# Queries and two gate blocks of a decoder layer's mixer as seven-product pairs, after keys and values

## The chip, the cores and the metric

One core of one Trainium2 chip runs a whole decoder layer as one program. The metric is the device time in microseconds, the median of several runs; a lower time is better. Inputs and output are float32, and the products keep nearly float32 accuracy by splitting each operand in two parts.

## The reference, cut to what matters

The layer is a feed-forward block, a token mixer, a cross-attention and a second feed-forward block on 256 tokens of width 2048. The change lies in the mixer:

```python
h = rms_norm(x, norm_g)                      # 256 x 2048
p = h @ w_in                                 # 2048 x (1024 + 512 + 3360 + 4096)
q, k, v, p_rwkv, gates = jnp.split(p, c, axis=-1)
y_attn = sliding_window_attention(q, k, v, sinks)
y_rwkv = rwkv7_time_mix(p_rwkv, ...)         # a recurrence over the tokens, 16 heads of 64
gate_attn, gate_rwkv = jnp.split(jax.nn.sigmoid(gates), 2, axis=-1)
merged = gate_attn * (y_attn @ w_proj_attn) + gate_rwkv * (y_rwkv @ w_proj_rwkv)
return x + merged @ w_out
```

## The kernel before, in words

**Products.** A product of the 256 tokens with a block of 512 columns goes over the inner dimension in chunks of 128 rows. Every weight chunk is split into `hi` (rounded by ScalarE to the matmul's format, line 365) and `lo` (the rest, VectorE, line 366), and the activations likewise (`xhi`, `xlo`). One elementary product is three matmuls, `hi`x`xhi`, `lo`x`xhi` and `hi`x`xlo` (`times`, lines 442 to 444), each 128 x 512. An *item* is two chunks (`KU`). A block of 2048 rows of weights (`product`) is 8 items, two token halves, 96 matmuls; a block of 1024 rows (`w_proj_attn`, `w_proj_rwkv`) is 4 items and 48 matmuls. Weights arrive by SyncE's DMA queue in `raw` tiles (four buffers) and are split two items ahead (`AHEAD`); a finished product is taken out of its `acc` banks (three) by ScalarE or VectorE.

**Seven products for eight.** In the feed-forward parts two column blocks are formed together (`product_pair`). A chunk pair of two blocks and two token halves is a 2 x 2 by 2 x 2 block product: eight elementary products, or seven by Winograd's scheme, of sums of weights (lines 394 to 397, split in lines 373 and 374) and of sums of activations (`combinations`). Three of eight chunk pairs of a feed-forward block use the seven. The partial results collect in the banks p1, p3, p5 (`mm`), p2, p4, q (`acc`) and p6, p7 (`tr`), which `first`, `middle` and `out` add up.

**The mixer.** Its products follow in a fixed order: two query blocks, keys and values, a small block of 288 columns ("small": decay, rate and gate inputs), two key blocks of the time-mixing branch (k0, k1), then four times an attention gate block and the `w_proj_attn` block it multiplies, then receptances and values (r0, v0, r1, v1), four gate blocks of the other branch (`gr`), four `w_proj_rwkv` blocks that read `yr`, and `w_out`.

**Background work.** Everything that isn't a product is a generator in one of eight groups (`Interleave`): `feat` turns results to features, `attn` holds eight `attend` jobs (two at a time), `ew` runs one job at a time and in order: `decay_and_rate`, `removal_keys` twice, `substitute` (inverts small triangular blocks, 31 steps on VectorE, lines 1187 and 1192), and then for each half `receptances` and `values`. `chain` holds four `pairs` jobs, two at a time: each waits for "inverse" (the end of `substitute`) and for "ready0" or "ready1" (the end of `values`), forms masked products (line 1290), goes through short dependent steps (lines 1327 to 1398) and hands its result to a `finish` job in `norm`: mean sums (line 875), square root, reciprocal (1445), gate matmuls (1457), four elementwise operations (1458 to 1465) and the split into `yrhi`, `yrlo` (635, 636). A product calls `bg.tick()` twice per item (`product_pair` about four times per item of two blocks), and a tick moves the running jobs by one step. A scheduler then places each engine's instructions, by their order of creation and what they depend on.

**Buffers.** Most tiles of the mixer share 23 buffers of 8 KB a partition (`t4`).

Of the kernel before, what the change touches and what calls it, by code (L numbers as in the profile page):

```python
# [7 lines left out]
F32 = mybir.dt.float32  # L8
# [7 lines left out]
P = 128  # L16
# [21 lines left out]

SEVEN, SEVEN_DOWN = (0, 2, 4), ((2, 4, 6), (2, 4))
SEVEN_2, STAGED = (0, 2, 3, 4), (3,)  # L40

STAGE_AT = [266 + 2 * n for n in range(10)]


class Act:
# [55 lines left out]
def weight_plan(a):  # L101

    w = {n: v[0] for n, v in a.items() if n in _INS}
    yield from feed_forward_plan(w["ffn1_w_gate"], w["ffn1_w_up"], w["ffn1_w_down"], False)
    yield None
    w_in = w["w_in"]
    cols = [0, 512, ATTN_W]
    for c in cols:  # L110
        yield w_in, 0, KD, c, 512
    yield w_in, 0, KD, C_RW + 3 * RW, 288
    for h in range(2):
        yield w_in, 0, KD, C_RW + RW + h * 512, 512
    for n in range(4):
        yield w_in, 0, KD, C_GATE + n * 512, 512
        yield w["w_proj_attn"], 0, 8, n * 512, 512
    for h in range(2):
        yield w_in, 0, KD, C_RW + h * 512, 512
        yield w_in, 0, KD, C_RW + 2 * RW + h * 512, 512  # L120
    for n in range(4):
        yield w_in, 0, KD, C_GATE + D + n * 512, 512
    for n in range(4):
        yield w["w_proj_rwkv"], 0, 8, n * 512, 512
    for n in range(4):
        yield w["w_out"], 0, KD, n * 512, 512
# [10 lines left out]
def decoder_layer(ctx: ExitStack, tc: tile.TileContext, a: dict, out: bass.AP):  # L137
# [19 lines left out]
    def f32(x):  # L157
        return x.bitcast(F32)
# [108 lines left out]

    plan, units, items, ends, staged = [], [], [], [], {}  # L270
    for entry in weight_plan(a):
        if entry is None:
            ends.append(len(units))
            continue
        plan.append(entry)
        w, k0, nk, c0, n = entry
        if not isinstance(w, tuple):
            for k in range(k0, k0 + nk, KU):
                items.append(((len(units),), False))
                units.append((w, k, c0, n))  # L280
            continue
        for k in range(k0, k0 + nk, 2 * KU):
            u = len(units)
            units += [(v, k + i, c, 512) for v, c in zip(w, c0) for i in (0, KU)]
            for i in range(2):
                q = (k - k0) // KU + i
                if n == SEVEN_2 and q in STAGED:
                    staged[len(items)] = len(staged)
                items.append(((u + i, u + 2 + i), q in n))
    raws, parts, summed = {}, {}, {}  # L290
    first_unused = {items[i][0][1] for i in staged}
    sums_d = dram.tile([len(staged), P, 4, 512], F32, name="sums")
    at = {"item": 0, "product": 0, "pool": None}

    def load(u, pieces=None):

        if u >= len(units) or u in raws:
            return
        w, k, c0, n = units[u]
        wide = at["pool"] is not None and (u < ends[0] or u >= ends[1] + LOADED)  # L300
        m = 2 if wide else 1
        if wide:
            raw = at["pool"].tile([P, m * KU, n], F32, tag="raw2", name="raw2", bufs=4)
        else:
            raw = wp.tile([P, KU, n], F32, tag="raw", name="raw", bufs=4)
# [62 lines left out]

    def two_parts(v, e):
        sp = at["pool"]  # L370
        hi = sp.tile([P, KU, 512], F32R, tag="thi" + e, name="thi")
        lo = sp.tile([P, KU, 512], F32R, tag="tlo" + e, name="tlo")
        act.copy(hi[:], v[:])  # L373
        dve.tensor_tensor(lo[:], v[:], f32(hi[:]), ALU.subtract)  # L374
        return hi, lo

    def divide(i):


        if i >= len(items) or i in parts:  # L380
            return
        which, seven = items[i]
        if len(which) == 1:
            parts[i] = split_unit(*which)
            return
        g, u = which
        if not seven:
            parts[i] = split_unit(g), split_unit(u)
            return
        t = summed.get(i)  # L390
        if t is None:
            rg, ru = raws[g], raws[u]
            t = [wp.tile([P, KU, 512], F32, tag="raw", name="raw", bufs=4) for _ in range(2)]
            dve.tensor_tensor(t[1][:, 0], ru[:, 0], rg[:, 0], ALU.subtract)
            dve.tensor_tensor(t[0][:, 0], ru[:, 1], ru[:, 0], ALU.subtract)
            dve.tensor_tensor(t[0][:, 1], ru[:, 1], t[1][:, 0], ALU.subtract)  # L396
            dve.tensor_tensor(t[1][:, 1], rg[:, 1], t[0][:, 1], ALU.subtract)
        a_ = two_parts(t[0], "a")
        parts[i] = split_unit(g), split_unit(u, slice(1, 2)), (a_, two_parts(t[1], "b"))

    def next_item():
        i = at["item"]
        at["item"] += 1
        u = items[i][0][0]
        for v in range(u, u + (2 * LOADED if at["pool"] is not None else LOADED)):
            load(v)
        divide(i)
        room = AHEAD
# [42 lines left out]
                k + i == 0, k + i == nk - 1,  # L451
            )

    def combinations(sp, x: Act, seven, name, ready=lambda: True, early=True, n=0):
# [5 lines left out]
        parts = [sp.tile([P, n, P], F32R, tag=name + e, name=name + e) for e in ("hi", "lo")]  # L460
        c = {"parts": parts, "at": {}, "done": False, "seven": seven, "early": early}

        def work():
# [3 lines left out]
            for q in pairs:  # L467
                while not {2 * q, 2 * q + 1} <= x.done:
                    yield
                t = wp.tile([P, KU, 512], F32, tag="raw", name="raw", bufs=4)  # L470
# [17 lines left out]
                s = slice(o, o + n)  # L488
                with tc.issue_after(at["hi"].ins):
                    act.copy(parts[0][:, s], f[:, :n])  # L490
                yield
                with tc.issue_after(at["lo"].ins):
                    dve.tensor_tensor(parts[1][:, s], f[:, :n], f32(parts[0][:, s]), ALU.subtract)
                c["at"][q] = o
                o += n
                yield
# [5 lines left out]
    def product_pair(x: Act, c, w, first, middle, out):  # L502
# [20 lines left out]
            return [x.at(p, k)[:, t * P : (t + 1) * P] for p in range(2)]  # L523

        def of_c(q, i):
            return [p[:, c["at"][q] + i, :] for p in c["parts"]]

        def of_w(parts_, i):
            return [p[:, i, :] for p in parts_]
# [246 lines left out]
    x3d = dram.tile([T, D], F32, name="x3d")  # L776
    md = dram.tile([T, D], F32, name="md")
    grd = dram.tile([T, D], F32, name="grd")
    ld = dram.tile([P, 32, P], F32, name="ld")
    xd = dram.tile([4, 32, 32, 32], F32, name="xd")  # L780

# [60 lines left out]
    with tc.tile_pool(name="mx", bufs=1, reuse_waits="tile") as sp:  # L842
# [39 lines left out]
                yield  # L882
            bg.seen.add(name)

        qt = []
        for h in range(2):
            tok = scaled(product(n2.x, W["w_in"]), n2.r)
            qt.append(t4("qt"))
            bg.spawn("feat", to_features(tok, qt[h], "q"))

        kd = t4("kd")
        vt = t4("vt", (P, 2, KV_W))
# [2 lines left out]
        for t in range(2):  # L895
# [6 lines left out]
            )  # L902
            act.activation(vt[:, t, :], pb[t][:, KV_W : 2 * KV_W], AF.Copy, scale=n2.r[t])
        bg.spawn("feat", to_features(tok, kd, "kv"))
        ya = act_tiles("ya", 2)
        sink4 = sinks[:].rearrange("p (k c e) -> p k e c", k=4, c=2)

        def attend(kv, qb):
            yield from wait_for("kv")
            w = P * (qb + 1)  # L910
            tq = slice(qb * P, qb * P + P)
            s = t4("s", (P, 2, 2, T))
# [289 lines left out]
        bg.spawn("ew", substitute())  # L1202


        for n in range(4):
            pg = product(n2.x, W["w_in"])
            g = t4("ga", (P, 2, 512))
            for t in range(2):
                act.activation(g[:, t, :], pg[t][:], AF.Sigmoid, scale=n2.r[t])
            pa = product(ya, W["w_proj_attn"])  # L1210
            for t in range(2):
                dve.tensor_tensor(g[:, t, :], pa[t][:], g[:, t, :], ALU.mult)
            pool.dma_start(blk(md, n), g[:])
# [503 lines left out]
```

## Time and profile before

| | |
|---|---|
| median of 3 runs | 2236.56 us (2236.5 to 2237.6) |
| the profiled execution, its own time | 2237.5 us |
| its span, first to last instruction | 2235.6 us |
| mean granted TensorE clock | 0.999 |
| matmuls (TensorE), longest group | 1134 x 3 `acc<-hi,xhi` and its two companions |

How to read the profile: PE is TensorE's matmuls, PEld its weight loads, DVE VectorE, ACT ScalarE, POOL GpSimd, SP SyncE, which issues the weight loads. `out<-in` names what an instruction writes and reads; `x1102` is a count, the next numbers are busy microseconds in all and mean nanoseconds of one. A matmul's row shows it from start to end, and successive matmuls overlap. Lines of `...` leave lines out. A line such as L443 is a line of the kernel before; in the kernel after, the same statements stand 2 to about 70 lines further down (443 is 456, 1290 is 1359, 1445 is 1514).

### The profile page before, as it was taken

How to read it: one execution, taken by the hardware profiler on the slowest of the kernel's cores; microseconds unless marked ns; L12 is line 12 of the kernel's file. 1: busy time of each engine (PE TensorE's matmuls, PEld its weight loads, DVE VectorE, ACT ScalarE, POOL GpSimd, SP SyncE). 2: the span in 40 equal slices, each digit the busy share in tenths (PEclk: the TensorE clock that was granted, in tenths of full speed). 3: DMA queues.
4: the chain of work that ended last, by engine and by line, in shares of the span. 5: the costliest groups of instructions: out<-in, count | busy, mean ns of one | idle time of the engine just before them, and what ended most of it. 6: DMA issues, size and time to landing. Idle time of an engine off the chain costs nothing.

```text
span 2235.6 us, 28143 instructions
## 1 busy us (share of the span) xinstructions
PE 2220.6 (99%) x10520; PEld 1823.4 (82%) x10520; DVE 1823.0 (82%) x2367; ACT 1247.3 (56%) x1625; POOL 121.3 (5%) x181
## 2 busy tenths in 40 slices
PE   9999999999999999999999999999999999999998
PEld 7888888888888877788888888888888888888886
DVE  7999989998989476977657666547999999999997
ACT  7555555555556467544434546556665565655654
POOL 0000000000001001200321030001000000000000
PEclk9999999999999999999999999999999999999999
DMA  8565565556556545687768688658565576556564
GB/s 303 194 210 197 188 209 201 193 190 214 199 189 199 172 134 152 196 232 212 206 215 279 196 260 283 187 160 275 200 243 201 193 242 210 203 206 222 198 227 150
DMA packets 231256, 466.02 MB, mean 208 GB/s; under 512 B 15472, under 2 KB 17616, under 8 KB 231120
## 3 DMA queue, kind: packets, MB, share of 16 engines
q1 hardware_dynamic: 221808, 437.56, 59.0%
q0 software_dynamic: 7648, 23.52, 3.5%
q10 hardware_dynamic: 1664, 3.15, 0.4%
q8 instruction: 82, 1.34, 0.3%
q14 instruction: 54, 0.44, 0.1%
HBM read 440.49 MB, written 23.59 MB: 208 GB/s over the span
## 4 chain that ended last, share of the span: by engine, by line
PE 93%; DVE 3%; DMA 2%; issue 1%; ACT 1%; POOL 0%; SPq 0%; POOLq 0%; ACTq 0%; DVEq 0%
PE acc L442 19%; PE acc L443 18%; PE acc L444 18%; PE mm L444 8%; PE mm L443 8%; PE mm L442 8%; PE tr L443 2%; PE tr L630 2%; PE tr L442 2%; PE tr L444 2%; DVE lo L366 1%; PE mm L1354 1%; PE tr L1290 1%; DMA raw<-in_ffn_w_up_dram 0%; PE mm L917 0%
## 5 line engine op out<-in xcount | busy, mean ns | idle before, releaser
L365 ACT CAST hi<-raw 128x1024 fp32r<-128x1024 f32 (+1 forms) x770 | 755.9, 992 | 701.8 <-PE acc L444 508.7
L366 DVE TENSOR_TENSOR lo<-raw,hi 128x1024 fp32r<-128x1024 f32 (+1 forms) x770 | 881.0, 1147 | 295.2 <-ACT hi L365 293.5
L442 PE MATMUL acc<-hi,xhi 128*128 128x512 f32 (+1 forms) x1134 | 448.3, 396 | 1.4 <-DVE xhi L661 0.6
L443 PE MATMUL acc<-lo,xhi 128*128 128x512 f32 (+1 forms) x1134 | 440.5, 388 | 1.1 <-DVE lo L366 1.1
L444 PE MATMUL acc<-hi,xlo 128*128 128x512 f32 (+1 forms) x1134 | 440.0, 388 | 0.0
L442 PEld LDWEIGHTS acc<-hi,xhi 128*128 128x128 f32 x1134 | 213.2, 188 | 48.5 <-issue 4.9
L443 PEld LDWEIGHTS acc<-lo,xhi 128*128 128x128 f32 x1134 | 213.1, 188 | 44.6 <-DVE lo L366 2.5
L444 PEld LDWEIGHTS acc<-hi,xlo 128*128 128x128 f32 x1134 | 212.9, 188 | 44.1 <-DVE xlo L664 0.5
L373 ACT CAST thi<-raw 128x1024 fp32r<-128x1024 f32 x192 | 199.7, 1052 | 65.3 <-DVE raw L396 44.8
L374 DVE TENSOR_TENSOR tlo<-raw,thi 128x1024 fp32r<-128x1024 f32 x192 | 232.0, 1217 | 1.3 <-ACT thi L373 0.6
L442 PE MATMUL mm<-hi,xhi 128*128 128x512 f32 x402 | 157.9, 393 | 0.1
L444 PE MATMUL mm<-hi,xlo 128*128 128x512 f32 x402 | 156.7, 390 | 0.0
L443 PE MATMUL mm<-lo,xhi 128*128 128x512 f32 x402 | 156.7, 390 | 0.0
L444 PE MATMUL acc<-hi,hlo 128*128 128x512 f32 x372 | 145.5, 391 | 0.0
L443 PE MATMUL acc<-lo,hhi 128*128 128x512 f32 x372 | 145.4, 391 | 0.0
L442 PE MATMUL acc<-hi,hhi 128*128 128x512 f32 x372 | 144.9, 390 | 0.0
L442 PEld LDWEIGHTS mm<-hi,xhi 128*128 128x128 f32 x402 | 75.5, 188 | 15.8 <-ACT hi L365 0.5
L444 PEld LDWEIGHTS mm<-hi,xlo 128*128 128x128 f32 x402 | 75.4, 188 | 15.8
L443 PEld LDWEIGHTS mm<-lo,xhi 128*128 128x128 f32 x402 | 75.5, 188 | 15.4
L443 PEld LDWEIGHTS acc<-lo,hhi 128*128 128x128 f32 x372 | 69.8, 188 | 14.3
L442 PEld LDWEIGHTS acc<-hi,hhi 128*128 128x128 f32 x372 | 69.9, 188 | 14.3
L444 PEld LDWEIGHTS acc<-hi,hlo 128*128 128x128 f32 x372 | 69.9, 188 | 14.0
(394 smaller groups left out, 3567.9 us busy)
## 6 DMA issues: line engine op xcount, KB each, us to landing
raw<-in_ffn_w_down_dram SPq DMA_DIRECT2D x88, 1024.0 KB, 5.2
raw<-in_ffn_w_gate_dram SPq DMA_DIRECT2D x84, 1024.0 KB, 5.2
raw<-in_ffn_w_up_dram SPq DMA_DIRECT2D x78, 1024.0 KB, 6.2
raw<-in_w_in_dram SPq DMA_DIRECT2D x136, 512.0 KB, 3.8
raw<-in_w_out_dram SPq DMA_DIRECT2D x32, 512.0 KB, 4.9
raw<-sums SPq DMA_DIRECT2D x20, 512.0 KB, 6.4
raw<-in_w_proj_attn_dram SPq DMA_DIRECT2D x16, 512.0 KB, 3.8
raw<-in_w_proj_rwkv_dram SPq DMA_DIRECT2D x16, 512.0 KB, 5.9
```

What stands on the lines that cost most here:

```text
L365: at["hi"] = act.copy(hi[:, s], raw[:, s])
L366: at["lo"] = dve.tensor_tensor(lo[:, s], raw[:, s], f32(hi[:, s]), ALU.subtract)
L373: act.copy(hi[:], v[:])
L374: dve.tensor_tensor(lo[:], v[:], f32(hi[:]), ALU.subtract)
L442: pe.matmul(o, xh, hi, start=first, stop=False, **how)
L443: pe.matmul(o, xh, lo, start=False, stop=False, **how)
L444: pe.matmul(o, xl, hi, start=False, stop=last, **how)
L630: pe.transpose(b[:, o : o + P], tok[:, t, col : col + P], ident[:])
L1290: pe.matmul(b[e][:, o : o + P], x1[r, j, cs_], x2[r, j, cs_], start=True, stop=True)
L1354: pe.matmul(vb[:, (o + k) * P : (o + k + 1) * P][:, r], lhs(k, e), rhs[:, k, r], start=first and k + e == 0, stop=True, **ek,)
```

## The change

The mixer's plan and program begin with the keys and values. Then the two query blocks, and after them the first two attention gate blocks, are formed as pairs with seven products for eight in chunk pairs 2, 4 and 6 of eight. The finished gate blocks are stored to memory (`gad`), and each is loaded again where its `w_proj_attn` block is due. The two other gate blocks stay products of one block, each ahead of one of the first two `w_proj_attn` blocks; the last two of these follow at once. Both pairs use combinations of the normalised activations (`cm`), weight sums (`tsum`), their splits and a second set of four load buffers (`raw3`), all kept in the 23 shared buffers for that time. Attention jobs wait for both query blocks. The points at which the second feed-forward block's staged sums are begun move by 16 items, the number of items that the two pairs save.

```diff
+SEVEN_MIX = (2, 4, 6)
-STAGE_AT = [266 + 2 * n for n in range(10)]
+STAGE_AT = [250 + 2 * n for n in range(10)]
...
-    cols = [0, 512, ATTN_W]
-    for c in cols:
-        yield w_in, 0, KD, c, 512
+    yield w_in, 0, KD, ATTN_W, 512
+    for c in (0, C_GATE):
+        yield (w_in, w_in), 0, KD, (c, c + 512), SEVEN_MIX
...
     for n in range(4):
-        yield w_in, 0, KD, C_GATE + n * 512, 512
+        if n < 2:
+            yield w_in, 0, KD, C_GATE + (2 + n) * 512, 512
         yield w["w_proj_attn"], 0, 8, n * 512, 512
...
+        elif u in mix_second:
+            raw = at["mix"]["raw"][sorted(mix_second).index(u) % 4]
...
-        qt = []
-        for h in range(2):
-            tok = scaled(product(n2.x, W["w_in"]), n2.r)
-            qt.append(t4("qt"))
-            bg.spawn("feat", to_features(tok, qt[h], "q"))
+        cm = combinations(sp, n2.x, SEVEN_MIX, "cm", early=False, n=12, room=room)
+
+        def pair_of(w, o, func, done):
+            def first(b):
+                act.copy(o[0][:, 0], b["p1"][:])
+            def middle(b):
+                dve.tensor_tensor(u2, b["p6"][:], o[0][:, 0], ALU.add)
+                dve.tensor_tensor(u3, b["p7"][:], u2, ALU.add)
+                dve.tensor_tensor(u2, b["p5"][:], u2, ALU.add)
+                dve.tensor_tensor(o[1][:, 1], b["q"][:], u3, ALU.add)
+            def out(b, to):
+                t, i = int(to in ("p4", "p5")), int(to in ("p3", "p5"))
+                v = o[i][:, t]
+                e = {"p2": v, "p4": u3, "p3": u2, "p5": v}[to]
+                dve.tensor_tensor(v, b[to][:], e, ALU.add)
+                act.activation(v, v, func, scale=n2.r[t])
+                if t:
+                    done(i)
+            product_pair(n2.x, cm, w, first, middle, out)
...
+        qt = [t4("qt") for _ in range(2)]
+        tok = [t4("tok", (P, 2, 512)) for _ in range(2)]
+        pair_of(W["w_in"], tok, AF.Copy,
+            lambda i: bg.spawn("feat", to_features(tok[i], qt[i], f"q{i}")))
+        ga = [t4("ga", (P, 2, 512)) for _ in range(2)]
+        pair_of(W["w_in"], ga, AF.Sigmoid,
+            lambda i: pool.dma_start(blk(gad, i), ga[i][:]))
...
             yield from wait_for("kv")
+            yield from wait_for("q1")
...
+        gates = []
         for n in range(4):
-            pg = product(n2.x, W["w_in"])
-            g = t4("ga", (P, 2, 512))
-            for t in range(2):
-                act.activation(g[:, t, :], pg[t][:], AF.Sigmoid, scale=n2.r[t])
+            if n < 2:
+                g = t4("ga", (P, 2, 512))
+                gates.append(g)
+                pool.dma_start(g[:], blk(gad, n))
+                pg = product(n2.x, W["w_in"])
+                g = t4("ga", (P, 2, 512))
+                gates.append(g)
+                for t in range(2):
+                    act.activation(g[:, t, :], pg[t][:], AF.Sigmoid, scale=n2.r[t])
             pa = product(ya, W["w_proj_attn"])
+            g = gates[(0, 2, 1, 3)[n]]
             for t in range(2):
                 dve.tensor_tensor(g[:, t, :], pa[t][:], g[:, t, :], ALU.mult)
             pool.dma_start(blk(md, n), g[:])
```

More of the change, by code (lines that the diff above doesn't have):

```diff
@@ L265, in decoder_layer @@
     junk_t = cpool.tile([P, 512], mybir.dt.bfloat16, name="junk")
-    plan, units, items, ends, staged = [], [], [], [], {}
+    plan, units, items, ends, staged, mix_second = [], [], [], [], {}, set()
     for entry in weight_plan(a):
@@ L289, in decoder_layer @@
                 items.append(((u + i, u + 2 + i), q in n))
+            if len(ends) == 1:
+                mix_second.update((u + 2, u + 3))
     raws, parts, summed = {}, {}, {}
@@ L292, in decoder_layer @@
     sums_d = dram.tile([len(staged), P, 4, 512], F32, name="sums")
-    at = {"item": 0, "product": 0, "pool": None}
+    at = {"item": 0, "product": 0, "pool": None, "mix": None}
     def load(u, pieces=None):
@@ L370, in two_parts @@
         sp = at["pool"]
-        hi = sp.tile([P, KU, 512], F32R, tag="thi" + e, name="thi")
-        lo = sp.tile([P, KU, 512], F32R, tag="tlo" + e, name="tlo")
+        if sp is None:
+            hi, lo = at["mix"][e]
+        else:
+            hi = sp.tile([P, KU, 512], F32R, tag="thi" + e, name="thi")
+            lo = sp.tile([P, KU, 512], F32R, tag="tlo" + e, name="tlo")
         act.copy(hi[:], v[:])
@@ L392, in divide @@
             rg, ru = raws[g], raws[u]
-            t = [wp.tile([P, KU, 512], F32, tag="raw", name="raw", bufs=4) for _ in range(2)]
+            if at["pool"] is None:
+                t = at["mix"]["t"]
+            else:
+                t = [wp.tile([P, KU, 512], F32, tag="raw", name="raw", bufs=4) for _ in range(2)]
             dve.tensor_tensor(t[1][:, 0], ru[:, 0], rg[:, 0], ALU.subtract)
@@ L404, in next_item @@
         u = items[i][0][0]
-        for v in range(u, u + (2 * LOADED if at["pool"] is not None else LOADED)):
+        deep = at["pool"] is not None or len(items[i][0]) == 2
+        for v in range(u, u + (2 * LOADED if deep else LOADED)):
             load(v)
@@ L452, in multiply, with combinations @@
             )
-    def combinations(sp, x: Act, seven, name, ready=lambda: True, early=True, n=0):
+    def combinations(sp, x: Act, seven, name, ready=lambda: True, early=True, n=0, room=None):
         pairs = [q for q in range(max(seven) + 1) if early or q in seven]
         n = n or sum(4 if q in seven else 2 for q in pairs)
-        parts = [sp.tile([P, n, P], F32R, tag=name + e, name=name + e) for e in ("hi", "lo")]
+        if room is None:
+            whole = [sp.tile([P, n, P], F32R, tag=name + e, name=name + e) for e in ("hi", "lo")]
+            parts = [lambda o, n, t=t: t[:, o : o + n] for t in whole]
+        else:
+            parts = [
+                lambda o, n, t=t: t[o // 8][:, o % 8 : o % 8 + n] for t in (room[:2], room[2:])
+            ]
         c = {"parts": parts, "at": {}, "done": False, "seven": seven, "early": early}
@@ L469, in work @@
                     yield
-                t = wp.tile([P, KU, 512], F32, tag="raw", name="raw", bufs=4)
+                if room is None:
+                    t = wp.tile([P, KU, 512], F32, tag="raw", name="raw", bufs=4)
+                else:
+                    t = at["mix"]["t4"]("ct", (P, KU, 512))
                 v = t[:, 0].rearrange("p (k t n) -> p k t n", k=2, t=2)
@@ L487, in work @@
                 yield
-                s = slice(o, o + n)
+                hi, lo = (v(o, n) for v in parts)
                 with tc.issue_after(at["hi"].ins):
-                    act.copy(parts[0][:, s], f[:, :n])
+                    act.copy(hi, f[:, :n])
                 yield
                 with tc.issue_after(at["lo"].ins):
-                    dve.tensor_tensor(parts[1][:, s], f[:, :n], f32(parts[0][:, s]), ALU.subtract)
+                    dve.tensor_tensor(lo, f[:, :n], f32(hi), ALU.subtract)
                 c["at"][q] = o
@@ L525, in of_c @@
         def of_c(q, i):
-            return [p[:, c["at"][q] + i, :] for p in c["parts"]]
+            return [p(c["at"][q] + i, 1)[:, 0] for p in c["parts"]]
         def of_w(parts_, i):
@@ L778, in decoder_layer @@
     grd = dram.tile([T, D], F32, name="grd")
+    gad = dram.tile([T, 2 * 512], F32, name="gad")
     ld = dram.tile([P, 32, P], F32, name="ld")
@@ L883, in to_features @@
             bg.seen.add(name)
-        qt = []
-        for h in range(2):
-            tok = scaled(product(n2.x, W["w_in"]), n2.r)
-            qt.append(t4("qt"))
-            bg.spawn("feat", to_features(tok, qt[h], "q"))
+        at["mix"] = {
+            "a": [t4("thi", (P, KU, 512), F32R), t4("tlo", (P, KU, 512), F32R)],
+            "b": [t4("thi", (P, KU, 512), F32R), t4("tlo", (P, KU, 512), F32R)],
+            "t": [t4("tsum", (P, KU, 512)) for _ in range(2)],
+            "raw": [t4("raw3", (P, KU, 512)) for _ in range(4)],
+            "t4": t4,
+        }
+        room = [t4("cm", (P, 8, P), F32R) for _ in range(4)]
+        u2, u3 = (t4("um", (P, 2, 512))[:, i] for i in range(2))
+        cm = combinations(sp, n2.x, SEVEN_MIX, "cm", early=False, n=12, room=room)
[16 more added lines that the diff above has]
+            product_pair(n2.x, cm, w, first, middle, out)
         kd = t4("kd")
@@ L904, in decoder_layer @@
         bg.spawn("feat", to_features(tok, kd, "kv"))
+        qt = [t4("qt") for _ in range(2)]
+        tok = [t4("tok", (P, 2, 512)) for _ in range(2)]
+        pair_of(
+            W["w_in"], tok, AF.Copy,
+            lambda i: bg.spawn("feat", to_features(tok[i], qt[i], f"q{i}")),
+        )
+        ga = [t4("ga", (P, 2, 512)) for _ in range(2)]
+        pair_of(
+            W["w_in"], ga, AF.Sigmoid,
+            lambda i: pool.dma_start(blk(gad, i), ga[i][:]),
+        )
         ya = act_tiles("ya", 2)
```

## The prediction

> **What bounds the kernel now.** I read the page first (busy time, slices, chain), then windows of 20 us, then the instructions of the stretch in which the time-mixing branch meets the merged projection.
>
> ```profile
> span 2235.6 us, 28143 instructions
> PE 2220.6 (99%) x10520; PEld 1823.4 (82%) x10520; DVE 1823.0 (82%) x2367; ACT 1247.3 (56%) x1625; POOL 121.3 (5%) x181
> DVE  7999989998989476977657666547999999999997
> DMA packets 231256, 466.02 MB, mean 208 GB/s; under 512 B 15472, under 2 KB 17616, under 8 KB 231120
> PE 93%; DVE 3%; DMA 2%; issue 1%; ACT 1%; POOL 0%; SPq 0%; POOLq 0%; ACTq 0%; DVEq 0%
> ```
>
> TensorE is busy 99% of the span and is 93% of the chain that ended last. So a matmul taken away shortens the kernel by its spacing, and a microsecond in which TensorE waits lengthens it by one. VectorE is full in the feed-forward parts and half empty in the mixer (slices 13 to 24, about 700 to 1340 us), where the change puts its work. The spacing is read where nothing but products run, at the seam from the last gate product to the first product on `yr`:
>
> ```profile
> 1288.41 0.39 PE L443 MATMUL acc<-lo,xhi 128*128 128x512 f32 x1
> 1288.64 0.39 PE L444 MATMUL acc<-hi,xlo 128*128 128x512 f32 x1
> 1288.87 0.39 PE L442 MATMUL acc<-hi,yrhi 128*128 128x512 f32 x1
> 1289.09 0.39 PE L443 MATMUL acc<-lo,yrhi 128*128 128x512 f32 x1
> ```
>
> Starts lie 0.2267 us apart (0.68 us for three), though each row is 0.39 us long: they overlap. The gate product runs straight into `yr`: nothing waits there now.
>
> ```profile
> core 0: us, PE busy (x) PEld busy (x) DVE busy (x) ACT busy (x) POOL busy (x), PEclk, DMA share, GB/s
> 220.00:240.00 20.00, 20.00 (x90) 16.57 (x89) 19.29 (x25) 10.22 (x11) 0.00 (x0) 1.00 0.56 189
> 740.00:760.00 20.00, 20.00 (x92) 16.54 (x91) 8.57 (x7) 9.03 (x11) 0.00 (x0) 1.00 0.66 186
> 800.00:820.00 20.00, 19.25 (x108) 13.86 (x107) 15.75 (x40) 13.87 (x41) 1.75 (x3) 1.00 0.39 120
> 1100.00:1120.00 20.00, 18.71 (x126) 15.38 (x126) 11.05 (x14) 9.34 (x14) 4.18 (x7) 1.00 0.88 279
> ```
>
> The first row is feed-forward with seven-for-eight pairs: VectorE 19.29 of 20 and TensorE still full. The second is a query product as it is now. The last two hold the idle time of attention (0.75 us) and of the start of the time-mixing chain (1.29 us).
>
> **Part 1, the matmuls removed: -4.1 us.** A chunk pair of two column blocks takes 8 x 3 matmuls, with seven products 7 x 3. Three chunk pairs in each of two pairs of blocks (queries, first gates): 2 x 3 x 3 = 18 matmuls, 18 x 0.2267 = 4.08 us. All are on TensorE's path; nothing else covers them.
>
> **Part 2, VectorE's work in the two pairs: no cost inside, 2.0 us at the seams.**
>
> ```profile
> L366 DVE TENSOR_TENSOR lo<-raw,hi 128x1024 fp32r<-128x1024 f32 x662 | 808.1, 1222 | 288.0 <-ACT hi L365 286.3
> L374 DVE TENSOR_TENSOR tlo<-raw,thi 128x1024 fp32r<-128x1024 f32 x192 | 232.0, 1217 | 1.3 <-ACT thi L373 0.6
> L366 DVE TENSOR_TENSOR lo<-raw,hi 128x512 fp32r<-128x512 f32 x100 | 68.1, 682 | 0.8 <-ACT hi L365 0.8
> L394 DVE TENSOR_TENSOR raw<-raw,raw 128x512 f32<-128x512 f32 x86 | 58.9, 685 | 13.3 <-DMA raw<-in_ffn_w_up_dram 12.7 <-DMA raw<-in_ffn_w_down_dram 0.3
> L581 DVE TENSOR_TENSOR u<-mm,u 128x512 f32<-128x512 f32 x20 | 13.6, 682 | 0.0
> ```
>
> A seven item is 4 x 0.685 + 2 x 1.217 + 1.222 + 0.682 = 7.1 us of VectorE, an eight item 2 x 1.222 = 2.4; three and five of them, with about ten additions from the banks at 0.682, are 40.3 us beside (5 x 24 + 3 x 21) x 0.2267 = 41.5 us of TensorE, 97%. Window 220 to 240 holds the same density, 96%, with TensorE full: inside a pair I charge nothing. If that cover went, 2 to 5 us a pair. The combinations of `n2.x` (nine long and twelve short operations, some 7 us) fall in the keys-and-values product, where VectorE is half idle. At the seams it is tighter: both pairs hold all three `acc` banks (p2, p4 and q), and the bank that the next product needs is freed in `middle`, three additions (2.05 us) after p5, with splits of 1.2 us between. Feed-forward pairs before have no q and start at once. Two seams, from nothing to 2 us each; I take 1 each.
>
> ACT (56% busy) and SP (the same number of 512 KB loads, 16 of them into `raw3`) have room. POOL gets four DMA issues, and 2 MB of store and reload is 0.4% of the 466 MB moved; all this is charged nothing, hidden by products of 21.8 us (96 x 0.2267). The new wait for "q1" costs nothing, since attention is queued behind the gate pair.
>
> **Part 3, what is moved: the time-mixing chain comes later, about 6.7 us.** This sets the sign. Background work advances by one step at each tick, and a product ticks twice an item: 16 times for 2048 rows of weights, 8 times for 1024. Group "ew" runs one job at a time: removal keys, then `substitute`, then `receptances` and `values`, and only behind those can `pairs` begin. From the second key product to the first receptance product there are 4 x 16 + 4 x 8 = 96 ticks now, and 2 x 16 + 4 x 8 = 64 after, because two gate products went ahead of the keys. So the chain comes 32 ticks nearer to its consumer.
>
> ```profile
> L1290 PE MATMUL tr<-at,aa x64: 272/272/373, 1104.7 to 1233.3; 64*128 64x128 f32 x64
> L442 PE MATMUL acc<-hi,yrhi x64: 387/389/482, 1288.9 to 1334.6; 128*128 128x512 f32 x64
> ```
>
> In the built order of instructions, 396 product matmuls stand between the first L1290 and the first `yrhi` product before, 228 after: 168 x 0.2267 = 38 us of cover gone. The end of the chain is what had slack:
>
> ```profile
> 1254.36 0.39 PE L1398 MATMUL tr<-mk,sa 128*64 128x128 f32 x4
> ...
> 1258.89 0.62 PE L875 MATMUL tr<-sp,ones_r 128*128 128x512 f32 x2
> 1259.54 0.69 ACT L1441 ACTIVATE sq<-tr,gneps 128x512 f32<-128x512 f32 x1 [0.76 <-PE tr L875]
> 1260.26 3.35 DVE L1445 RECIPROCAL sq<-sq 128x512 f32<-128x512 f32 x1 [0.23 <-ACT sq L1441]
> 1263.42 0.40 PE L1457 MATMUL tr<-xr,gh 128*128 128x256 f32 x2
> 1263.53 1.16 DVE L366 TENSOR_TENSOR lo<-raw,hi 128x1024 fp32r<-128x1024 f32 x1
> 1264.36 0.39 PE L442 MATMUL acc<-hi,xhi 128*128 128x512 f32 x1
> 1264.61 0.68 DVE L1458 TENSOR_TENSOR yq<-yq,sq 128x512 f32<-128x512 f32 x1
> 1264.69 1.28 ACT L1487 ACT_TABLE_LOAD   x1
> 1265.21 1.22 DVE L366 TENSOR_TENSOR lo<-raw,hi 128x1024 fp32r<-128x1024 f32 x1
> 1266.34 0.87 DVE L1462 SCALAR_TENSOR_TENSOR yq<-yq,cols,bv 128x256 f32<-128x256 f32 x2
> 1267.13 0.86 DVE L1465 SCALAR_TENSOR_TENSOR yq<-yq,cols,tr 128x256 f32<-128x256 f32 x2
> 1268.03 0.62 ACT L635 CAST yrhi<-yq 128x512 fp32r<-128x512 f32 x1
> 1268.68 0.69 DVE L636 TENSOR_TENSOR yrlo<-yq,yrhi 128x512 fp32r<-128x512 f32 x1 [0.69 <-ACT yrhi L635]
> ```
>
> From the last mean sums (L875) to the last `yrlo` is 1269.37 - 1258.89 = 10.5 us, two splits of 1.16 and 1.22 us among them. Bare it is 0.62 + 0.69 + 3.35 + 0.68 + 0.87 + 0.86 + 0.62 + 0.69 = 8.4 us. Before, 162 product matmuls (36.7 us) stand between these sums and the product that reads this block of `yr`. After, the built order has only the sums (0.45 us), the eight gate matmuls of L1457 (0.94 us, 1263.42 to 1264.36) and six product matmuls (1.36 us): 2.75 us. TensorE then waits for `yrhi`, 8.4 - 0.7 - 2.75 = 4.95 us, and after two matmuls some 0.25 for `yrlo`: 5.2 us, or 7.3 if two splits get in again. The built order shows none between the reciprocal and `yrlo`, so I take 5.2. The block before it has about 11 us of cover for a path of the same length plus a table load (1.28) and two splits (2.4), which makes a wait near 0.75; the chain's last copies and the first merged transposes behind it add as much. I take 1.5 for these (0 to 3).
>
> At the start of the chain, the 1.29 us idle at 1100 to 1120 may go or come back (-1.2 to +1.2): nothing charged.
>
> Sum: -4.1 + 2.0 + 5.2 + 1.5 = +4.6 us, so 2242.1 against the profiled execution's 2237.5; the median of the runs is 0.94 lower, so **2241.2 us**.
>
> TensorE's clock column reads 1.00 in every window above, and the worst of them loses 1.3 us in all. The Trainium skill, "TensorE: Matmul & The Clock Gate", section "What's actually happening", says that the array falls to half clock after an idle window of about 3.4 us and needs a busy one as long to come back. By that rule the new 5 us wait would cost an estimated further 1.7 us; no run here shows a pause that long.
>
> **Rivals.** (a) The other side: the tail is covered. If `ready0` came early enough that the last sums stood 40 product matmuls before their consumer (9 us, more than 8.4), no wait arises and the 18 matmuls are all: 2236.6 - 4.1 + (0 to 2) = 2233.5, below 2232.1 only if attention's 0.75 or the chain start's 1.29 us go too. For it: TensorE is full at 1280 to 1300 now. Against: six matmuls in the built order. 15%. (b) VectorE becomes the bound in the two pairs: at 97% any handover between ACT and VectorE (286 us of waits on L365 in all) pushes it over; the first pair also carries the 7 us of combinations. 5 us more: 2246. Against: window 220 to 240. 13%. (c) After the wait the matmuls run slower: twelve of them at double spacing are 2.7 us, half of that 1.4; 2 us more: 2243.2. For it only the length of the pause. 7%. The clock page's rule is this case. (d) The waits just eat the gain, with seams at nothing and the start of the chain smoother: 2237, 5%.
>
> **How the numbers follow.** Forecast 60%, its own range 2238.5 to 2244, a little more than half above +0.2% (2241.0); 0.2% either way is about what a measurement of this kernel tells from no change. Slower: 0.33 + 0.13 + 0.07 = 0.53. Within: 0.27 + 0.07 of (a) + 0.05 = 0.39. Faster: 0.08, the rest of (a). Range: low, tail at 5.2, everything else at its lower end with some of (a), 2235; high, tail 7.3, seams 4, others 3, 2247 with (b).
>
> **What would show it.** Right: eighteen fewer 128x512 matmuls; a TensorE pause of 4 to 8 us before the third and fourth chunk pairs of the first product on `yr`, ended by ACT's `yrhi`; L1290's first start some 35 us later; TensorE full in both pairs. Wrong: no such pause (a); pauses on `lo` or `tlo` inside the pairs (b); PEclk under 1.00 behind the pause (c). A time under 2235 would say that the tail was covered.

## The result, and the profile after

The kernel after takes 2265.45 us (median of 4 runs, 2264.92 to 2268.81) against 2236.61 us before in the same runs: a ratio of 1.0131, 95% interval 1.0114 to 1.0149, or 28.8 us slower. The forecast was 2241.2 us (2235 to 2247): slower was right, the size was not.

From the page of the kernel after (span, busy time, slices, the chain that ended last):

```profile
span 2263.6 us, 28202 instructions
...
PE 2229.4 (98%) x10502; PEld 1826.6 (81%) x10502; DVE 1868.3 (83%) x2437; ACT 1257.1 (56%) x1642; POOL 127.9 (6%) x185
...
PE 91%; DMA 3%; DVE 3%; issue 1%; ACT 1%; POOL 1%; SPq 0%; POOLq 0%; DVEq 0%; ACTq 0%
```

The 18 matmuls are gone (10502 for 10520). The span grew by 28.0 us though TensorE has less to do, so the time is in gaps. To place them, take the starts of successive matmuls: what lies beyond the usual (median) distance for the first one's shape is *excess*. By stretches of the span, in us:

| stretch (us) | before | after | difference |
|---|---|---|---|
| 712 to 800, the mixer's opening and the pairs | 1.8 | 5.5 | +3.7 |
| 800 to 1100 | 5.9 | 5.8 | -0.1 |
| 1100 to 1180, ahead of and at the chain's start | 1.9 | 19.6 | +17.7 |
| 1180 to 1300, within the chain | 1.7 | 4.3 | +2.6 |
| 1300 to 1340, the products on `yr` | 0.2 | 8.0 | +7.8 |
| all others | 14.7 | 14.9 | +0.2 |
| matmuls removed | | | -4.1 |

Together 27.8 us. The same three windows, first of the kernel before, then of the kernel after:

```profile
core 0: us, PE busy (x) PEld busy (x) DVE busy (x) ACT busy (x) POOL busy (x), PEclk, DMA share, GB/s
1104.00:1130.00 26.00, 24.71 (x186) 20.99 (x185) 18.50 (x26) 11.18 (x18) 4.67 (x7) 1.00 0.81 270
1130.00:1180.00 50.00, 50.00 (x384) 44.12 (x383) 26.50 (x35) 22.21 (x38) 15.03 (x24) 1.00 0.68 218
1320.00:1330.00 10.00, 10.00 (x48) 8.27 (x47) 6.30 (x7) 4.59 (x5) 4.18 (x3) 1.00 0.82 289
```

```profile
1104.00:1130.00 26.00, 26.00 (x126) 21.74 (x125) 21.17 (x28) 10.02 (x11) 3.46 (x2) 1.00 0.99 352
1130.00:1180.00 50.00, 38.67 (x162) 28.54 (x161) 30.41 (x38) 13.76 (x17) 12.54 (x19) 0.83 0.99 349
1320.00:1330.00 10.00, 5.11 (x15) 3.72 (x14) 5.91 (x8) 0.62 (x1) 0.95 (x1) 0.66 0.18 54
```

In 1130 to 1180 TensorE is idle for 11.3 us and its granted clock is 0.83; no compute engine is near its limit, but the 16 DMA engines are 99% busy, where before they had 68%. The last window holds the forecast pause on `yr`, with DMA at 18%: another cause.

Who waited for what in 1130 to 1180 after the change (total, times, longest), then its DMA issues (count, size, median time to landing), then the same issues before:

```profile
ACT hi L371 <- DMA raw<-in_w_in_dram: 33.0, 8, 9.4
...
PEld acc L455 <- ACT hi L371: 11.0, 4, 5.7
PE acc L455 <- ACT hi L371: 9.6, 3, 5.3
...
POOL rb L1333 <- DMA sums<-su: 6.8, 2, 4.3
```

```profile
raw<-in_w_in_dram SPq DMA_DIRECT2D x10, 512.0 KB, 10.5
sums<-su SPq DMA_DIRECT2D x6, 512.0 KB, 10.2
sums<-sg SPq DMA_DIRECT2D x5, 512.0 KB, 10.5
su<-in_ffn_w_up_dram SPq DMA_DIRECT2D x4, 512.0 KB, 6.5
sg<-in_ffn_w_gate_dram SPq DMA_DIRECT2D x3, 512.0 KB, 6.5
```

```profile
raw<-in_w_in_dram SPq DMA_DIRECT2D x7, 512.0 KB, 4.7
su<-in_ffn_w_up_dram SPq DMA_DIRECT2D x4, 512.0 KB, 6.0
sg<-in_ffn_w_gate_dram SPq DMA_DIRECT2D x4, 512.0 KB, 7.3
sums<-su SPq DMA_DIRECT2D x3, 512.0 KB, 3.5
sums<-sg SPq DMA_DIRECT2D x3, 512.0 KB, 4.1
```

TensorE waits for `hi`, ScalarE, which makes `hi`, waits 33 us in all for weights, and a 512 KB weight load takes 10.5 us to land in place of 4.7. The last wait shows the chain itself held up: POOL waits 6.8 us for staged stores to land before it may write `rb`, a tile of the chain in the shared buffers. Of the DMA issues listed, 18 are the *staging* of the second feed-forward: ten groups (`STAGE_AT`) that each load 1 MB (`su`, `sg`), form sums, and store 1 MB (`sums`). Their place among the products did not change; the chain's did. First starts in the kernel before (attention's scores, the staged stores), then after (scores, the chain's first masked products, the staged stores):

```profile
L917 PE MATMUL mm<-kd,qt x64: 272/375/480, 784.5 to 832.9; 64*128 64x128 f32 x32, 64*128 64x256 f32 x32
...
L358 SPq DMA_DIRECT2D sums<-su x10: 319/339/413, 1115.6 to 1240.5; - x10
```

```profile
L979 PE MATMUL mm<-kd,qt x64: 272/374/480, 827.6 to 874.0; 64*128 64x128 f32 x32, 64*128 64x256 f32 x32
...
L1359 PE MATMUL tr<-at,aa x64: 272/272/373, 1147.9 to 1293.2; 64*128 64x128 f32 x64
...
L364 SPq DMA_DIRECT2D sums<-su x10: 338/382/779, 1106.3 to 1198.3; - x10
```

Attention and chain both start 43 us later (784.5 to 827.6, 1104.7 to 1147.9), about the time of the gate pair that now stands ahead of them (41.5 us in Part 2). The staged stores went over 125 us beside the chain, whose small matmuls stretch the time between two weight items; now they go over 92 us, 42 of them ahead of the chain, where products run at full rate and ask for weights most often.

### The profile page after: what moved, and what is told of

Its sections match the earlier page's. It is cut to its first block, busy times and chain, and to the rows that moved or that the text cites. A ratio compares the mean times of both kernels' runs of the same rounds, so it can differ in the third digit from the quotient of the medians.

```text
span 2263.6 us, 28202 instructions
## 1 busy us (share of the span) xinstructions
PE 2229.4 (98%) x10502; PEld 1826.6 (81%) x10502; DVE 1868.3 (83%) x2437; ACT 1257.1 (56%) x1642; POOL 127.9 (6%) x185
## 4 chain that ended last, share of the span: by engine, by line
PE 91%; DMA 3%; DVE 3%; issue 1%; ACT 1%; POOL 1%; SPq 0%; POOLq 0%; DVEq 0%; ACTq 0%
PE acc L455 17%; PE acc L456 17%; PE acc L457 17%; PE mm L456 8%; PE mm L455 8%; PE mm L457 8%; PE tr L456 2%; DMA raw<-in_w_in_dram 2%; PE tr L455 2%; PE tr L457 2%; PE tr L652 2%; PE mm L1423 1%; DVE lo L372 1%; PE tr L1359 1%; DMA sums<-su 1%
## 5 line engine op out<-in xcount | busy, mean ns | idle before, releaser
L371 ACT CAST hi<-raw 128x1024 fp32r<-128x1024 f32 (+2 forms) x770 | 753.0, 988 | 709.8 <-PE acc L457 461.5
L372 DVE TENSOR_TENSOR lo<-raw,hi 128x1024 fp32r<-128x1024 f32 (+2 forms) x770 | 880.0, 1147 | 269.2 <-ACT hi L371 267.0
L455 PE MATMUL acc<-hi,xhi 128*128 128x512 f32 (+1 forms) x1068 | 423.5, 398 | 10.8 <-ACT hi L371 9.6
L456 PE MATMUL acc<-lo,xhi 128*128 128x512 f32 (+1 forms) x1068 | 418.4, 392 | 4.3 <-DVE lo L372 4.1
L457 PE MATMUL acc<-hi,xlo 128*128 128x512 f32 (+1 forms) x1068 | 416.7, 390 | 0.0
L455 PEld LDWEIGHTS acc<-hi,xhi 128*128 128x128 f32 x1068 | 201.7, 189 | 56.5 <-ACT hi L371 11.0
L457 PEld LDWEIGHTS acc<-hi,xlo 128*128 128x128 f32 x1068 | 202.3, 189 | 41.6 <-issue 0.3
L455 PE MATMUL mm<-hi,xhi 128*128 128x512 f32 x432 | 169.9, 393 | 0.2 <-DVE um L927 0.2
L456 PE MATMUL mm<-lo,xhi 128*128 128x512 f32 x432 | 168.5, 390 | 0.7 <-DVE lo L372 0.7
L457 PE MATMUL mm<-hi,xlo 128*128 128x512 f32 x432 | 168.6, 390 | 0.0
```

Source lines behind the costliest of these rows:

```text
L371: at["hi"] = act.copy(hi[:, s], raw[:, s])
L372: at["lo"] = dve.tensor_tensor(lo[:, s], raw[:, s], f32(hi[:, s]), ALU.subtract)
L455: pe.matmul(o, xh, hi, start=first, stop=False, **how)
L456: pe.matmul(o, xh, lo, start=False, stop=False, **how)
L457: pe.matmul(o, xl, hi, start=False, stop=last, **how)
```

## The experiments

The kernel before, timed beside them, took 2236.8 us (first four) and 2237.3 us (the others). The diffs show the lines that matter; `...` leaves lines out.

**Staging 7 items later** (`stage_later`).

```diff
-STAGE_AT = [250 + 2 * n for n in range(10)]
+STAGE_AT = [257 + 2 * n for n in range(10)]
```

> Kernel after, with the staging of the second feed-forward's sums begun 7 items (some 38 us of products) later, nothing else changed. Theory A (the staging's loads and stores fall on the products ahead of the time-mixing chain, DMA is saturated there and weights come late): the excess of TensorE's time between 1100 and 1180 us, 19.6 us after against 1.9 before, falls under 5 us, the DMA share there under 0.95, and the time is 2265.4 - 14 to 17 = 2248 to 2252 us; the pause before the last yr product (5 us) stays. Theory B (the late chain itself holds TensorE, whatever is staged): 2262 to 2268 us with the same pauses at 1137 to 1172 us.

2261.08 us (ratio 1.0106, 1.0091 to 1.0121): 4.4 us better, where A wanted 14 to 17, and 1 us under B's range. A miss: the excess from 1130 to 1180 fell from 19.5 to 12.3 only, with DMA still at 95% in that window. The first staged sum was formed at 1123 us, still 22 us ahead of the chain's start (1145.6); in the kernel before it came 6 us behind it. So 7 items were too few to tell A from B. Of the windows there, after the edit:

```profile
1130.00:1180.00 50.00, 44.01 (x238) 35.85 (x237) 29.03 (x38) 13.78 (x20) 11.74 (x18) 0.88 0.95 325
```

**The kernel before, staging 7 items earlier** (`before_stage_early`).

```diff
-STAGE_AT = [266 + 2 * n for n in range(10)]
+STAGE_AT = [259 + 2 * n for n in range(10)]
```

> Kernel before, with the staging begun 7 items earlier, so that it runs ahead of the chain as it does after the change. Theory A: weights come late in the 45 us ahead of the chain, 2236.6 + 8 to 16 = 2245 to 2253 us, DMA share over 0.95 there. Theory B (staging has nothing to do with it): 2235.5 to 2238 us.

2245.77 us (1.0042, 1.0026 to 1.0058), 9 us slower, in A's range. The windows ahead of and at the chain's start:

```profile
1080.00:1104.00 24.00, 24.00 (x120) 20.12 (x119) 21.69 (x29) 10.88 (x14) 11.80 (x17) 1.00 0.93 305
1104.00:1130.00 26.00, 21.46 (x137) 17.60 (x136) 15.39 (x20) 9.26 (x14) 3.92 (x6) 0.87 0.96 327
```

DMA share 0.93 and 0.96, TensorE 4.5 us idle: one number gives the kernel before a loss of the same kind, about half as large (excess 9.2 us from 1100 to 1180, where the kernel after has 19.6). It did not fall quite as A said. Ahead of the chain TensorE lost nothing (24.00 of 24), and its longest pause, 4.0 us up to 1114.0, was at the chain's start, for VectorE's `mk`; VectorE had just waited 1.3 us for a staged store to land. Weights were late as well: ScalarE waited 8.5 us for one, up to 1117.4.

**The query pair alone** (`q_pair_only`): gates and order as before, but keys and values first.

```diff
-STAGE_AT = [250 + 2 * n for n in range(10)]
+STAGE_AT = [258 + 2 * n for n in range(10)]
...
-    for c in (0, C_GATE):
-        yield (w_in, w_in), 0, KD, (c, c + 512), SEVEN_MIX
+    yield (w_in, w_in), 0, KD, (0, 512), SEVEN_MIX
...
-        if n < 2:
-            yield w_in, 0, KD, C_GATE + (2 + n) * 512, 512
+        yield w_in, 0, KD, C_GATE + n * 512, 512
...
```

> Kernel after with the gate pair undone: keys and values, the query pair, then everything in the order of before; staging begun 8 items earlier than before, the items that one pair saves. Theory A (the loss is the later chain, which the gate products ahead of attention cause): attention and chain stand where they stood before, no pause on staging and none on yr; the query pair saves 9 x 0.227 = 2.0 us and keeps the opening's excess of up to 3.7 us: 2234.5 to 2239 us. Theory C (seven-product pairs are too dense for VectorE in the mixer): about half of the loss stays, 2245 to 2252 us.

2240.48 us (1.0016, 1.0007 to 1.0026), 1.5 us above A's range and far from C's. The excess is no larger than before at the chain's start (0.8, before 1.9) and on `yr` (0.2); the opening keeps 5.4.

**The order without pairs** (`order_only`).

```diff
-STAGE_AT = [250 + 2 * n for n in range(10)]
+STAGE_AT = [266 + 2 * n for n in range(10)]
...
-    for c in (0, C_GATE):
-        yield (w_in, w_in), 0, KD, (c, c + 512), SEVEN_MIX
+    for c in (0, 512, C_GATE, C_GATE + 512):
+        yield w_in, 0, KD, c, 512
...
```

> Order of after without any seven-product pair: keys and values, two single query products, two single gate products (stored and loaded again), then as after; staging at the items of before, which is the same place among the products as after. Theory A (order): the same losses as after at the chain's start and on yr, 17.7 + 2.6 + 7.8 us, without the 4.1 us saved and without the opening's 3.7: 2258 to 2268 us. Theory C (pairs): 2236 to 2241 us.

2264.26 us (1.0122, 1.0101 to 1.0142). A: excess of 20.1 from 1100 to 1180 and 8.2 on `yr`, with not one seven-product pair in the mixer. The window at the chain's start:

```profile
1130.00:1180.00 50.00, 36.48 (x161) 27.37 (x160) 29.38 (x38) 12.95 (x16) 12.56 (x19) 0.90 1.00 342
```

The loss is the order's. C falls.

**Staging 26 and 14 items later** (`stage_after_chain`, then `stage_in_chain`).

```diff
-STAGE_AT = [250 + 2 * n for n in range(10)]
+STAGE_AT = [276 + 2 * n for n in range(10)]
...
+STAGE_AT = [264 + 2 * n for n in range(10)]
```

> Kernel after with the staging begun 26 items later, so that most of it falls behind the chain's start; nothing else changed. Moving it 7 items gave only 4.4 us, with DMA still at 104% of a stretch of 20 us and a memset on POOL waiting for a store of staged sums. Theory A (staging's DMAs next to the chain's start): the excess of 12.3 us that was left between 1130 and 1180 us falls under 4, the time to 2265.4 - 15 to 18 = 2247 to 2251 us, and only the opening (3.7) and the pauses on yr (8) are left beside the 4.1 saved. Theory B (the chain's own start, its gathers and the gate stores): 2257 to 2262 us.

> Kernel after with the staging begun 14 items later than there: between stage_later (7, which still met the chain's start) and stage_after_chain (26, where the chain's start ran without a wait but the staging met the products on yr, 11.4 us of excess there instead of 8.0 and 6.2 instead of 2.5 ahead of them). Theory: the excess between 1130 and 1180 us stays under 3 and that on yr goes back to 8: 2265.4 - 16.5 to 18.5 = 2247 to 2249 us, still some 10 slower than before by the pauses on yr and the opening. Rival (the staging only moves its cost about): 2252 us or more.

The first took 2255.01 us (1.0078, 1.0058 to 1.0098), 4 us above A and 2 under B. Its two windows, at the chain's start and on `yr`:

```profile
1130.00:1180.00 50.00, 49.69 (x346) 42.68 (x345) 22.93 (x27) 19.58 (x30) 13.35 (x23) 1.00 0.52 142
...
1300.00:1340.00 40.00, 31.36 (x133) 24.12 (x133) 32.49 (x40) 12.32 (x14) 10.01 (x9) 0.91 0.84 302
```

The chain's start is clean (excess -0.4), so its own gathers and gate stores cost nothing: B falls. But the staging now meets the products on `yr` (DMA share 1.03 from 1320 to 1340), where the excess rose to 11.4. The second keeps clear of both:

```profile
1130.00:1180.00 50.00, 48.35 (x313) 40.99 (x311) 28.48 (x37) 18.52 (x27) 13.91 (x23) 1.00 0.83 253
...
1300.00:1340.00 40.00, 34.03 (x152) 27.23 (x151) 27.56 (x28) 14.58 (x18) 13.11 (x11) 0.91 0.54 182
```

2248.48 us (1.0048, 1.0034 to 1.0061), as forecast: excess 2.1 and 8.1. The place of the staging is worth 2265.4 - 2248.5 = 17 us of the 28.8. Against the kernel before, what is left is some 3.4 us at the opening, 3.4 within the chain and 7.9 on `yr`, less the 4.1 saved.

**Attention ahead of the gates** (`attention_before_gates`): `order_only` with the `attend` jobs begun before the two gate products.

```diff
+        for kv in range(4):
+            for qb in range(2):
+                bg.spawn("attn", attend(kv, qb))
         for n in range(2):
             pg = product(n2.x, W["w_in"])
...
-        for kv in range(4):
-            for qb in range(2):
-                bg.spawn("attn", attend(kv, qb))
```

> The order-only kernel with the attention jobs begun ahead of the two gate products instead of behind them. Two theories of what makes the chain late: keys formed later (my step: fewer ticks between the keys and the receptances), or attention begun later, on which the decay waits. In the built order the chain's first masked product stands 12 us earlier than in the order-only kernel and still 27 us later than before, so both have a part. The last mean sums stand 8 us earlier: cover 2.7 + 8.2 = 10.9 us against a path of 8.4, so the 5 us pause on yr should go, and the staging meets the chain's start half as much: 2264.3 - 8 - 5 to 13 = 2243 to 2251 us. If only keys count: 2260 us or more. If only attention counts: 2236 to 2239 us.

2246.52 us (1.0040, 1.0024 to 1.0056). The chain's first products, and the stretch of the products on `yr`:

```profile
L1326 PE MATMUL tr<-at,aa x64: 272/272/373, 1132.0 to 1266.2; 64*128 64x128 f32 x64
```

```profile
1300.00:1340.00 40.00, 40.00 (x190) 33.14 (x189) 27.12 (x30) 17.64 (x21) 14.01 (x11) 1.00 0.83 267
```

The chain starts at 1132.0, 13 us earlier than in `order_only` (1145.1) and 27 later than before (1104.7). So of the 40 us there, attention, on which the decay waits, makes 13; the other 27 go with the gate products that stand ahead of the keys, since `q_pair_only`, which has them behind the keys, starts its chain at 1106.3. The pause on `yr` is gone (excess 0.2 for 8.2), and the chain's start loses 8.1 for 20.1.

**Three tries at a faster version.** `kv_first` changes the kernel before, the two others change `q_pair_only`; the three edits in this order:

```diff
-    cols = [0, 512, ATTN_W]
+    cols = [ATTN_W, 0, 512]
...
             while not ready():
                 yield
+            if room is not None:
+                yield from idle(4)
...
-SEVEN_MIX = (2, 4, 6)
+SEVEN_MIX = (4, 6)
```

> Kernel before with the keys and values ahead of the two query products, nothing else. The order-only kernel showed an opening excess of 0.3 us between 712 and 800 us where before shows 1.8. If that comes from this order alone: 2236.8 - 1.5 = 2235.3 us; if not: 2236.5 to 2237.5 us.

> The query-pair-only kernel with the combinations of the activations begun four ticks (some 11 us) later. There, in the keys-and-values product, TensorE waited 1.7 us at 733 us for a weight split that stood behind two combinations on VectorE. Theory: that pause and the 0.3 before it go: 2240.5 - 2 = 2238 to 2239 us. Rival (the combinations now push back the splits of the pair itself): 2240 to 2243 us.

> The query-pair-only kernel with seven products in chunk pairs 4 and 6 alone: two combinations in place of three, three matmuls (0.68 us) more. If the combinations cause the opening's pause of 1.7 us at 733 us, it falls under 0.6 and the opening's excess from 5.4 to about 4; the 1.0 us at the seam into the pair (741 us) stays, since the seam is there without them. Time within 1 us of the 2240.5 of that kernel. If the pause stays, it is the constants on POOL that hold ScalarE.

`kv_first` took 2237.66 us (1.0002, 0.9993 to 1.0012): no gain. `q_pair_combos_later` took 2242.85 us (1.0023, 1.0014 to 1.0033), the rival: the pause at 733 us fell from 1.67 to 0.18, but new ones of 0.7 and 0.8 came at 738 and one of 1.5 at 742, early in the pair, and behind them the matmuls ran at half rate from 745.3 to 748.7 (1.4 us more). `q_pair_two_sevens` took 2237.64 us (1.0000, 0.9990 to 1.0010). The window 730 to 735 of `q_pair_only`, then of this kernel:

```profile
730.00:735.00 5.00, 3.37 (x14) 2.43 (x14) 5.00 (x14) 2.35 (x4) 0.00 (x0) 1.00 0.35 105
```

```profile
730.00:735.00 5.00, 4.84 (x20) 3.39 (x19) 4.96 (x10) 2.45 (x3) 0.00 (x0) 1.00 0.67 208
```

VectorE is full in both; with one combination less TensorE has 1.5 us more. The pause at 733 us fell to 0.21, the 1.0 at the seam went too, and the opening's excess is 3.4: the combinations cause the pause. The forecast of the seam was wrong; since the pair's first seven-product item now comes two items later, the run does not tell whether the combinations or that item made the 1.0 us. It is as fast as before, not faster.

**The kernel before, staging 5 items later** (`before_stage_later`).

```diff
-STAGE_AT = [266 + 2 * n for n in range(10)]
+STAGE_AT = [271 + 2 * n for n in range(10)]
```

> Kernel before with the staging begun 5 items later, behind the chain's start, where TensorE waits 1.1 us at 1111.4 for VectorE, which waits for a staged load. Theory: that wait goes and nothing comes for it, 2237.3 - 1.1 = 2236.2 us. Rival (it meets the products on yr, or TensorE's order has another wait there): 2237 to 2239 us.

2242.46 us (1.0022, 1.0013 to 1.0031), slower than either theory: pauses of 2.66 us at 1178.7 and 1.7 at 1271.3, in stretches of 20 us with DMA shares of 0.90 and 0.92. No version beat the kernel before.

## Why the prediction was wrong

**The step that failed** is the account of DMA: the end of Part 3 charged nothing for the chain's start (-1.2 to +1.2 us), and Part 2 counted for DMA only what the change adds (four issues, 2 MB of store and reload), not what it moves together. What it adds did cost nothing: from 800 to 1100 us, where the store and reload fall, the excess is 5.9 before and 5.8 after. But the staging keeps its place among the products while the chain moves back, and this cost 17.7 us at the chain's start. The quoted window 1100 to 1120 already had DMA at 0.88, and in it VectorE waited 1.2 us for a staged load, just ahead of the `mk` that ended TensorE's longest wait (0.97 us): that was the row to follow. No rival held this case. That the kernel would be slower was forecast for a reason that held, the pause on `yr`: with the staging out of the way (`stage_in_chain`) 11.2 us are lost, for 4.6 forecast.

**Matmuls removed, -4.1:** right, 10502 for 10520.

**Seams and opening, +2.0:** measured +3.7. Inside the pairs it was right and rival (b) wrong: 760 to 780 us after the change, in the first pair, has TensorE at 20.00 of 20 and VectorE at 16.29, and 800 to 820, in the second, TensorE at 20.00 and VectorE at 15.20. What was mis-sized is the combinations, put into a product "where VectorE is half idle": in `q_pair_only` VectorE has no idle time from 730 to 735 us. A wait of ScalarE in the kernel after, for a constant from POOL, ends at 728.0 us, some 5 us ahead of the pause (total, times, longest):

```profile
ACT ones_r L236 <- POOL bdones L227: 4.2, 1, 4.2
```

so that splits and combinations come in a lump. It does not make the pause by itself: it is 4.2 us in `q_pair_two_sevens` too, where taking one combination away was enough to end the pause. Whether it adds to it was not tried. This pause (1.7) and the seam at 741 us (1.0) are most of the 3.7.

**The chain later, +6.7 on `yr`:** the mechanism was right and the size nearly so, 7.8, though partly from other terms than forecast. The last block in the kernel after:

```profile
1316.63 0.39 PE L898 MATMUL tr<-sp,ones_r 128*128 128x512 f32 x1
...
1317.69 1.22 DVE L372 TENSOR_TENSOR lo<-raw,hi 128x1024 fp32r<-128x1024 f32 x1 [2.88 <-ACT hi L371]
...
1318.83 3.34 DVE L1514 RECIPROCAL sq<-sq 128x512 f32<-128x512 f32 x1
...
1318.97 0.50 PE L456 MATMUL acc<-lo,yrhi 128*128 128x512 f32 x1 [0.76 <-DVE lo L372]
...
1320.02 0.40 PE L457 MATMUL acc<-hi,yrlo 128*128 128x512 f32 x1
...
1324.63 0.62 ACT L657 CAST yrhi<-yq 128x512 fp32r<-128x512 f32 x1 [6.40 <-DVE yq L1534]
1325.28 0.69 DVE L658 TENSOR_TENSOR yrlo<-yq,yrhi 128x512 fp32r<-128x512 f32 x1 [0.68 <-ACT yrhi L657]
...
1325.30 0.80 PE L455 MATMUL acc<-hi,yrhi 128*128 128x512 f32 x1 [4.89 <-ACT yrhi L657]
...
1325.90 0.63 PE L456 MATMUL acc<-lo,yrhi 128*128 128x512 f32 x1
...
1328.88 0.41 PE L457 MATMUL acc<-hi,yrlo 128*128 128x512 f32 x1
```

Six product matmuls follow the gate matmuls, then TensorE pauses for 1325.30 - 1320.02 - 0.23 = 5.05 us (forecast 4.95), and 0.37 more for `yrlo` (0.25). That the pause came so near is partly luck. A weight split got in (ScalarE's `hi`, then `lo` at 1317.69), which the forecast had left out. It held back the square root and the reciprocal, so the path from the first sums (1316.40) to the end of `yrhi` (1325.25) took 8.85 us in place of 7.7; and it held TensorE for 0.94 us among the six matmuls, so the pause also began later. The block before it waited 0.22 us for its `yrhi` (0.75 forecast). Rival (c) came true on top of it: behind 1325.90 seven starts, up to 1328.88, lie 0.426 us apart, 7 x 0.2 = 1.4 us more. The rule from the Trainium skill's "TensorE: Matmul & The Clock Gate" ("What's actually happening") agrees here in size: some 3.6 us at half clock behind a 5 us pause. The Trainium skill's idle window of about 3.4 us was not needed elsewhere: half clock also followed shorter pauses (last section), and there the measurement decides. The chain's delay was put down to ticks between keys and receptances alone (35 us); it is 43, and attention, begun behind the gates, had 13 of the 40 in `order_only`.

Were weights late because DMA could move no more, or because they stand behind staged transfers in SyncE's order? The trace of the kernel after shows both. From 1114 to 1136 us SyncE's 512 KB transfers landed one after another in the order of issue, 1.33 us apart (395 GB/s). Two weight items bring two weight loads and a group of staging four transfers, 6 x 1.33 = 8.0 us, while the 24 matmuls of two items take 24 x 0.2267 = 5.4 us: at full rate the products outrun this queue. Before the change a group came every 125 / 9 = 13.9 us. Then the order: SyncE waited 5.9 and 3.4 us, up to 1162.1, for staged stores to land before it could issue two staged loads, and issued no weight load between 1149.3 and 1162.57:

```profile
1162.09 0.38 SPq L352 DMA_DIRECT2D sg<-in_ffn_w_gate_dram  x1
...
1162.57 0.94 SPq L323 DMA_DIRECT2D raw<-in_w_in_dram  x2
```

The first of these weights landed at 1170.0, and TensorE's longest pause there (5.3 us) ended at 1171.2. The Trainium skill, "Perfetto Trace Analysis", section "Roofline", puts the limit of one core's 16 DMA engines at about 435 GB/s; the 50 us window here averages 349 at a share of 0.99, and small gathers (740 of its 7521 packets are under 512 B) are among them. What is not settled is how the loss divides between the two: neither weights ahead of the staging in SyncE's order nor fewer staged bytes was tried. The 2.6 us within the chain were not traced to a cause.

## What to carry to other kernels

When an edit delays a stage, list what keeps its old place, prefetches and staged copies above all, and add up the DMA shares of what now falls together; a share of 0.88 in one window left no room here (0.99 after the change, with late weights). Background transfers that are pinned to a count of items belong beside the stage whose small work slows the items, and they move with it. The built order of the instructions showed where the pause on `yr` would come, and, partly by luck, its size; where the staging stands beside the chain can be looked for in it in the same way.

## What the runs showed of the hardware

The granted clock also fell behind short pauses. In the kernel after, TensorE at the chain's start:

```profile
1137.25 0.39 PE L457 MATMUL acc<-hi,xlo 128*128 128x512 f32 x1
1139.33 0.74 PE L455 MATMUL acc<-hi,xhi 128*128 128x512 f32 x2 [1.69 <-ACT hi L371]
...
1141.56 0.63 PE L456 MATMUL acc<-lo,xhi 128*128 128x512 f32 x1
...
1144.81 0.39 PE L457 MATMUL acc<-hi,xlo 128*128 128x512 f32 x1
```

After 1.69 us of idle time the matmuls go on at full rate for some 2 us, then at half rate (0.43 us apart) until 1144.5; the granted clock is 0.53 from 1141.0 to 1144.5. In `q_pair_combos_later` the same followed an idle time of 1.37 us up to 743.3, with shorter ones just ahead of it. Idle times of about this length did nothing elsewhere: 1.55 us up to 735.3 in the kernel after, 1.85 up to 996.3 in `attention_before_gates`. So a pause's length alone does not decide it.
